# A float32 decoder trunk on one core: another order for the moving operand, and weights moved by 128 bytes

## Chip, cores and metric

The kernel runs on one core of one Trainium2 chip. The metric is the device time of one execution in microseconds, as the median of several runs; lower is better.

## The reference

Two decoder layers over 512 tokens of width 1,024, in float32. Each layer is a token mixer followed by a dense MLP with a squared ReLU, both behind an RMSNorm and added to the residual; one more RMSNorm ends it.

```python
def reference(x, ...):
    for i in range(DEPTH):                       # DEPTH = 2
        h = rmsnorm(x, norm_mix_g[i])
        if i % 2 == 0:  h = chunked_spatial_gating(h, ...)   # in: 1024 -> 2 x 2048, out: 2048 -> 1024
        else:           h = retention(h, ...)                # q, k: 4 heads x 256; v, g: 4 x 512; out: 2048 -> 1024
        x = x + h
        h = rmsnorm(x, norm_ffn_g[i])
        a = jax.nn.relu(h @ mlp_w1[i])                       # 1024 -> 4096
        x = x + (a * a) @ mlp_w2[i]                          # 4096 -> 1024
    return rmsnorm(x, final_norm_g)
```

## The kernel before

**Three matmuls for one product.** Every float32 operand is split into a high part of type float32r and the remainder, `lo = value - hi`. A product is then high x high + high x low + low x high, three matmuls into the same accumulator in PSUM. `mm3` (L213) issues them; L215, L216 and L217 are its lines. With 128 rows, 128 stationary columns and 512 moving columns each, nearly all of TensorE's time is in these three lines.

**Two directions.** Where the result is wanted with features on the partitions (`feat`, `out_piece`: groups `up` and `dn` in layer 1, `u`, `g`, `qk`, `o`, `ro`), the weights are the stationary operand, loaded 128 columns at a time, and 512 tokens of activation move. Where tokens are wanted on the partitions (`tokens`: groups `v`, `vv` and, in the second layer's last products, `dt`), activations are stationary and 512 columns of weights move. In the retention head, `sc` (scores) and `av` (scores times values) have activations on both sides, and 512, 384, 256 or 128 moving columns. Column sums for the norms and their spread over partitions (`stats`, `spread`: groups `st_...`, `bc_...`) have a constant, `onesr`, as the stationary operand and call `matmul` directly. So do the first four pieces of weights (`v0`, L562) and the small transposes (`xt`, `wst`, `tt`) and gating products (`sg`).

**Weights.** All weight matrices are cut into 240 pieces of 128 x 1,024 elements, in the order of use. The queue of SyncE brings in two pieces with a DMA of 1 MB into a `raw` tile. ScalarE copies a piece into `wH` (L179) and VectorE subtracts into `wL` (L183). `prep` does this two to three pieces ahead of TensorE; there are four `wH` tiles, three `wL` tiles and two `raw` tiles. `refill` calls it after each step, so VectorE's and ScalarE's queues hold this work between the evacuations of accumulators. The order of everything is written out by hand as a list of steps.

**Where things lie.** Tiles are allocated one behind another in each partition: the pool `keep` (constants, norms, `xT`, and the normed activations `hH`, `hL`), then `wts` (`raw`, `wH`, `wL`), `bigp` (other activations, ten tiles of 8 KB), `work`. In the built kernel `keep` begins at byte 16,512, `onesr` lies at 17,024, and a tile named `fill`, which nothing uses, puts `xT0` at 24,576. From there on `hH`, `hL`, the weights' tiles and `bigp`'s lie on multiples of 2,048. Both parts of a piece start at the start of their tile.

Of the kernel before, what the change touches and what calls it, by code (L numbers as in the profile page):

```python
# [10 lines left out]
F32 = mybir.dt.float32  # L11
F32R = mybir.dt.float32r
# [5 lines left out]
P = 128  # L18
# [60 lines left out]
def trunk(ctx, tc, x, norm_mix_g, norm_ffn_g, a_w_in, a_b_in, a_v_norm_g, a_w_s, a_b_s, a_w_out,  # L79
# [4 lines left out]
    keep = ctx.enter_context(tc.tile_pool(name="keep", bufs=1))  # L84
    wts = ctx.enter_context(tc.tile_pool(name="wts", bufs=3))
# [28 lines left out]
    ident = keep.tile([P, P], F32, name="ident")  # L114
    onesr = keep.tile([P, P], F32R, name="onesr")
    rows = keep.tile([P, P], F32, name="rows")
    rows2 = keep.tile([16, P], F32, name="rows2")
    gT = keep.tile([P, 80], F32, name="gT")
    wide = keep.tile([P, D], F32, name="wide")
    rbc, r2bc = wide[:, 0:T], wide[:, T:D]  # L120
    r4 = keep.tile([P, NT], F32, name="r4")
    rh4 = keep.tile([P, NT], F32, name="rh4")
    vgh = keep.tile([P, 16], F32, name="vgh")
# [3 lines left out]
    ssf = keep.tile([P, NT, 2], F32, name="ssf")  # L127
    ms0 = keep.tile([P, NT], F32, name="ms0")

    keep.tile([P, 320], F32, name="fill")  # L130
    xT = [keep.tile([P, T], F32, name=f"xT{k}") for k in range(KD)]
    hH = [keep.tile([P, T], F32R, name=f"hH{k}") for k in range(KD)]
    hL = [keep.tile([P, T], F32R, name=f"hL{k}") for k in range(KD)]
# [32 lines left out]

    def prep_tiles(i):
        p = order[i]
        p.hi = wts.tile(p.shape, F32R, tag="wH", name=f"wH{i}", bufs=4)
        p.lo = wts.tile(p.shape, F32R, tag="wL", name=f"wL{i}", bufs=3)  # L170

    def prep(upto, low=None):

        low = upto if low is None else low
        while pos["piece"] < min(upto, len(order)):
            p = order[pos["piece"]]
            load_raws(raws.index(p.raw) + RAW_BUFS)
            prep_tiles(pos["piece"])
            nc.scalar.copy(out=p.hi, in_=p.raw.tile[p.view])  # L179
            pos["piece"] += 1  # L180
        while pos["low"] < min(low, len(order)):
            p = order[pos["low"]]
            nc.vector.tensor_sub(out=p.lo, in0=p.raw.tile[p.view], in1=f32(p.hi))  # L183
            pos["low"] += 1
# [27 lines left out]

    def mm3(ps, ah, al, bh, bl, start, stop):  # L213

        nc.tensor.matmul(ps, lhsT=ah, rhs=bh, start=start, stop=False)  # L215
        nc.tensor.matmul(ps, lhsT=ah, rhs=bl, start=False, stop=False)  # L216
        nc.tensor.matmul(ps, lhsT=al, rhs=bh, start=False, stop=stop)  # L217
# [85 lines left out]
    def mm_f(p, ps, bH, bL, ks, last):  # L303
        for k in ks:
            mm3(ps, p.hi[:, k, :], p.lo[:, k, :], bH[k], bL[k], k == 0, k == last)

    def mm_o(p, t, ps, bH, bL):
        ts = slice(t * P, (t + 1) * P)
        for k in range(4):
            mm3(ps, p.hi[:, k, ts], p.lo[:, k, ts], bH[:, k, :], bL[:, k, :], k == 0, k == 3)  # L310
# [28 lines left out]
    def tokens(plist, bufs, evac, name, behind=None, last=None):  # L339

        accs = {}
        behind = behind or {}

        def one(i):
            def run(p):
                if i == 0:
                    for n in range(NT):
                        accs[n] = acc(f"{name}_{n}")
                aH, aL = bufs()
                for n in range(NT):  # L350
                    s = slice(n * P, (n + 1) * P)
                    for k in range(2):
                        kk = 2 * i + k
                        mm3(accs[n], aH[kk][:, s], aL[kk][:, s], p.hi[:, k, :], p.lo[:, k, :], kk == 0, kk == 7)
                advance()
                refill()
                if i in behind:
                    behind[i]()
                if i == 3:
                    for n in range(NT):  # L360
                        launch(evac(n, accs[n]))
            return run

        for i, p in enumerate(plist[:2] if last else plist):
            step(one(i), p)
        if last:
            step(lambda *ps: last(bufs, accs, evac, *ps), *plist[2:])
# [589 lines left out]
    for _ in range(5):  # L957
        nc.tensor.matmul(warm[:, 0:P], lhsT=ident, rhs=ident, start=True, stop=True)
    columns(rows2, 0, 16)
    prep_tiles(0)  # L960
    for k in range(2):
        p = order[0]
# [56 lines left out]
```

## Time and profile before

| | |
|---|---|
| median of 3 runs | 1406.9 us (1406.83 to 1407.25) |
| the profiled execution | 1407.72 us, of which the span from first to last instruction 1406.0 us |
| granted TensorE clock in it | 0.998 |
| TensorE matmul busy | 1390.5 us (99%) |
| weight loads busy | 1155.4 us (82%) |
| VectorE, ScalarE, GpSimd busy | 793.0, 507.2, 127.7 us |

How to read the rows below: PE is TensorE's matmul row, PEld its weight loads, DVE VectorE, ACT ScalarE, POOL GpSimd, SP SyncE. A row names the line of the kernel, what is written and from what, and the shapes. A matmul's start is measured; its end is modelled, and one starts before the one ahead of it has ended. What a stream of matmuls costs is therefore the distance between starts, not the length of one. A time in front of a row is from the start of the span.

### The profile page before, as it was taken

To read this page: it belongs to the slowest core of one execution; us is meant where nothing else is said; L and a number is where in the kernel's file an instruction comes from. 1 tells how busy PE (TensorE), PEld (TensorE's weight loads), DVE (VectorE), ACT (ScalarE), POOL (GpSimd) and SP (SyncE) were. 2 spreads that over 40 slices of the span, in tenths; PEclk is the share of its full clock that TensorE was granted. 3 is DMA by queue.
4 is the path that set the end of the run, shared out by engine and by line. 5 is a ranking of instruction groups with operands and counts; after the bars stand their busy time and mean duration, and the time that the engine had idled before them with its cause. 6 is when DMAs were issued, how large, how long until landed. Compare 5 with 4: busy or idle time off the path is not lost.

```text
span 1406.0 us, 15372 instructions
## 1 busy us (share of the span) xinstructions
PE 1390.5 (99%) x6290; PEld 1155.4 (82%) x6290; DVE 793.0 (56%) x1102; ACT 507.2 (36%) x721; POOL 127.7 (9%) x98
## 2 busy tenths in 40 slices
PE   8999999999999999999999999999999999999997
PEld 7888888888888888888888888888888888888885
DVE  6757765775444445476647574564685443434335
ACT  4656633334413223123334323333334422313222
POOL 3010111220000000011111100110130000000002
PEclk9999999999999999999999999999999999999999
DMA  6332222232223322423222131132122332232221
GB/s 225 109 116 90 72 90 88 81 120 90 90 90 104 106 90 90 148 89 108 90 78 72 60 120 60 62 118 90 61 90 91 120 104 90 93 117 91 90 90 60
DMA packets 106101, 135.23 MB, mean 96 GB/s; under 512 B 2400, under 2 KB 79792, under 8 KB 105776
## 3 DMA queue, kind: packets, MB, share of 16 engines
q1 hardware_dynamic: 106000, 134.26, 29.4%
q8 instruction: 49, 0.80, 0.2%
q14 instruction: 20, 0.16, 0.0%
q10 hardware_dynamic: 32, 0.01, 0.0%
HBM read 132.16 MB, written 2.10 MB: 95 GB/s over the span
## 4 chain that ended last, share of the span: by engine, by line
PE 96%; DVE 3%; POOL 0%; ACT 0%; DMA 0%; issue 0%; SPq 0%; ACTq 0%; DVEq 0%
PE up L217 8%; PE up L216 8%; PE up L215 8%; PE dn L217 4%; PE dn L216 4%; PE dn L215 4%; PE dt L216 4%; PE dt L217 4%; PE dt L215 4%; PE g L215 2%; PE qk L215 2%; PE vv L216 2%; PE g L216 2%; PE vv L215 2%; PE g L217 2%; PE vv L217 2%
## 5 line engine op out<-in xcount | busy, mean ns | idle before, releaser
L183 DVE TENSOR_TENSOR wL<-raw,wH 128x1024 fp32r<-128x1024 f32 x239 | 305.9, 1282 | 112.8 <-PE dt L216 65.5
L179 ACT CAST wH<-raw 128x1024 fp32r<-128x1024 f32 x239 | 249.7, 1045 | 264.7 <-PE dt L217 114.9
L215 PE MATMUL up<-hH,wH 128*128 128x512 f32 x480 | 187.2, 390 | 0.0
L217 PE MATMUL up<-hH,wL 128*128 128x512 f32 x480 | 186.8, 389 | 0.0
L216 PE MATMUL up<-hL,wH 128*128 128x512 f32 x480 | 186.8, 389 | 0.0
L631 DVE TENSOR_TENSOR aH<-r 128x512 fp32r<-128x512 f32 x64 | 45.0, 703 | 159.5 <-ACT r L629 159.4
L216 PEld LDWEIGHTS up<-hL,wH 128*128 128x128 f32 x480 | 90.1, 188 | 18.7
L215 PEld LDWEIGHTS up<-hH,wH 128*128 128x128 f32 x480 | 90.1, 188 | 18.7
L217 PEld LDWEIGHTS up<-hH,wL 128*128 128x128 f32 x480 | 90.1, 188 | 18.7
L215 PE MATMUL dn<-aH,wH 128*128 128x512 f32 x256 | 99.6, 389 | 0.0
L216 PE MATMUL dn<-aL,wH 128*128 128x512 f32 x256 | 99.6, 389 | 0.0
L217 PE MATMUL dn<-aH,wL 128*128 128x512 f32 x256 | 99.6, 389 | 0.0
L215 PE MATMUL dt<-wH,aH 128*128 128x512 f32 x256 | 99.6, 389 | 0.0
L216 PE MATMUL dt<-wL,aH 128*128 128x512 f32 x256 | 99.6, 389 | 0.0
L217 PE MATMUL dt<-wH,aL 128*128 128x512 f32 x256 | 99.6, 389 | 0.0
L629 ACT ACTIVATE r<-up 128x512 f32<-128x512 f32 x60 | 35.9, 598 | 166.7 <-PE up L217 166.7
L239 POOL TENSOR_TENSOR ssq<-ssq,sq 128x512 f32<-128x512 f32 x28 | 43.0, 1537 | 401.6 <-ACT sq L238 401.3
L501 DVE TENSOR_TENSOR xs<-dn,wide 128x512 f32<-128x512 f32 x32 | 22.1, 692 | 74.5 <-PE dn L217 74.5
L215 PEld LDWEIGHTS dt<-wH,aH 128*128 128x128 f32 x256 | 48.0, 188 | 10.1
L216 PEld LDWEIGHTS dn<-aL,wH 128*128 128x128 f32 x256 | 48.0, 188 | 10.0
L215 PEld LDWEIGHTS dn<-aH,wH 128*128 128x128 f32 x256 | 48.0, 188 | 10.0
L216 PEld LDWEIGHTS dt<-wL,aH 128*128 128x128 f32 x256 | 48.0, 188 | 9.9
(271 smaller groups left out, 2709.5 us busy)
## 6 DMA issues: line engine op xcount, KB each, us to landing
raw<-in_mlp_w_dram SPq DMA_DIRECT2D x64, 1024.0 KB, 5.1
raw<-in_b_w_in_dram SPq DMA_DIRECT2D x24, 1024.0 KB, 5.0
raw<-in_a_w_in_dram SPq DMA_DIRECT2D x14, 1024.0 KB, 5.2
raw<-in_a_w_out_dram SPq DMA_DIRECT2D x8, 1024.0 KB, 4.9
raw<-in_b_w_out_dram SPq DMA_DIRECT2D x8, 1024.0 KB, 4.9
raw<-in_a_w_in_dram SPq DMA_DIRECT2D x8, 256.0 KB, 6.7
out_dram<-out SPq DMA_DIRECT2D x8, 256.0 KB, 2.1
xr<-in_x_dram SPq DMA_DIRECT2D x3, 512.0 KB, 6.6
```

What stands on the lines that cost most here:

```text
L179: nc.scalar.copy(out=p.hi, in_=p.raw.tile[p.view])
L183: nc.vector.tensor_sub(out=p.lo, in0=p.raw.tile[p.view], in1=f32(p.hi))
L215: nc.tensor.matmul(ps, lhsT=ah, rhs=bh, start=start, stop=False)
L216: nc.tensor.matmul(ps, lhsT=ah, rhs=bl, start=False, stop=False)
L217: nc.tensor.matmul(ps, lhsT=al, rhs=bh, start=False, stop=stop)
L239: nc.gpsimd.tensor_tensor(out=state["ssq"], in0=state["ssq"], in1=sq, op=ALU.add)
L501: nc.vector.tensor_mul(t, ps, r2bc)
L629: nc.scalar.activation(r, ps, AF.Relu)
L631: nc.vector.tensor_mul(h, r, r)
```

## The change

In `mm3`, where the moving operand has 512 columns, the access patterns of the moving operand and of the output get two more levels: 64 groups, 2 halves, 4 columns. Columns pass in the order 0 to 3, 256 to 259, 4 to 7, 260 to 263 and so on: 16 bytes from the first 1,024 bytes of a row, 16 from the second. The output is addressed in the same order, so each column's result is where it was.

`wH` and `wL` tiles become 64 elements longer, 4,352 bytes in all, and a piece's part stands in the middle, 32 elements or 128 bytes from the tile's start. To make room, `rows2` (used once at the start, for turning the norms' gains) becomes a view of `wide`, and `fill` shrinks from 320 to 192 elements. With that `xT`, `hH` and `hL` begin 1,024 bytes earlier, `xT0` at 23,552, a multiple of 1,024; the weights' tiles, and `bigp` at 119,552, lie on multiples of 256.

```diff
-    rows2 = keep.tile([16, P], F32, name="rows2")
...
     rbc, r2bc = wide[:, 0:T], wide[:, T:D]
+    rows2 = wide[0:16, 0:P]
...
-    keep.tile([P, 320], F32, name="fill")
+    keep.tile([P, 192], F32, name="fill")
...
     def prep_tiles(i):
         p = order[i]
-        p.hi = wts.tile(p.shape, F32R, tag="wH", name=f"wH{i}", bufs=4)
-        p.lo = wts.tile(p.shape, F32R, tag="wL", name=f"wL{i}", bufs=3)
+        hi = wts.tile([P, 1024 + 64], F32R, tag="wH", name=f"wH{i}", bufs=4)
+        lo = wts.tile([P, 1024 + 64], F32R, tag="wL", name=f"wL{i}", bufs=3)
+        p.hi, p.lo = (t[:, 32 : 32 + 1024].rearrange("p (a b) -> p a b", a=p.shape[1]) for t in (hi, lo))
...
     def mm3(ps, ah, al, bh, bl, start, stop):
+        if bh.shape[1] == 512:
+            ps, bh, bl = (v.rearrange("p (h l f) -> p l h f", h=2, f=4) for v in (ps, bh, bl))
         nc.tensor.matmul(ps, lhsT=ah, rhs=bh, start=start, stop=False)
         nc.tensor.matmul(ps, lhsT=ah, rhs=bl, start=False, stop=False)
         nc.tensor.matmul(ps, lhsT=al, rhs=bh, start=False, stop=stop)
```

## The prediction

> **What bounds the kernel now.** I read the page first: the busy times, the chain that ended last, the costliest groups.
>
> ```profile
> span 1406.0 us, 15372 instructions
> PE 1390.5 (99%) x6290; PEld 1155.4 (82%) x6290; DVE 793.0 (56%) x1102; ACT 507.2 (36%) x721; POOL 127.7 (9%) x98
> PE 96%; DVE 3%; POOL 0%; ACT 0%; DMA 0%; issue 0%; SPq 0%; ACTq 0%; DVEq 0%
> L183 DVE TENSOR_TENSOR wL<-raw,wH 128x1024 fp32r<-128x1024 f32 x239 | 305.9, 1282 | 112.8 <-PE dt L216 65.5
> L179 ACT CAST wH<-raw 128x1024 fp32r<-128x1024 f32 x239 | 249.7, 1045 | 264.7 <-PE dt L217 114.9
> L215 PE MATMUL up<-hH,wH 128*128 128x512 f32 x480 | 187.2, 390 | 0.0
> ```
>
> TensorE (PE) is the chain: 96% of it. No other engine is near its limit over the whole. So the question is what one matmul costs. The 390 ns of the group row is the modelled length of one, not its price: they overlap. The price is the distance between two starts, which the timeline shows, with the weight loads of the same stretch behind it:
>
> ```profile
> 499.98 0.39 PE L217 MATMUL dn<-aH,wL 128*128 128x512 f32 x1
> 500.20 0.39 PE L215 MATMUL dn<-aH,wH 128*128 128x512 f32 x1
> 500.43 0.39 PE L216 MATMUL dn<-aL,wH 128*128 128x512 f32 x1
> 500.66 0.39 PE L217 MATMUL dn<-aH,wL 128*128 128x512 f32 x1
> ...
> 500.43 0.19 PEld L217 LDWEIGHTS dn<-aH,wL 128*128 128x128 f32 x1
> 500.66 0.19 PEld L215 LDWEIGHTS dn<-aH,wH 128*128 128x128 f32 x1
> ```
>
> Three starts take 0.68 us, 226.7 ns each, and the load for the next matmul begins with the present one, every time. The same over long stretches, in the view that cuts the span into windows (length, PE busy, count; then PEld, DVE, ACT, POOL; clock, DMA share, GB/s):
>
> ```profile
> 314.00:652.00 338.00, 338.00 (x1492) 279.79 (x1491) 177.72 (x217) 103.69 (x132) 12.73 (x8) 1.00 0.31 103
> 1010.00:1098.00 88.00, 87.96 (x404) 72.91 (x404) 64.26 (x90) 37.99 (x56) 11.95 (x8) 1.00 0.32 102
> ```
>
> 338.00 us over 1,491 loads is 226.7 ns a matmul, though the stretch mixes weights that are a piece of the matrix with moving activations, from several pools.
>
> How much of 226.7 ns is the 512 columns? The retention head has matmuls of fewer columns in one run:
>
> ```profile
> 716.68 0.39 PE L215 MATMUL av<-pH,vvH 128*128 128x512 f32 x1
> ...
> 717.36 0.33 PE L215 MATMUL av<-pH,vvH 128*128 128x384 f32 x1
> ...
> 717.88 0.29 PE L215 MATMUL av<-pH,vvH 128*128 128x256 f32 x1
> ...
> 718.25 0.22 PE L215 MATMUL av<-pH,vvH 128*128 128x128 f32 x1
> ```
>
> Three matmuls of 512 columns take 0.68 us, three of 384 take 0.52, three of 256 take 0.37. From 512 to 384 that is (680 - 520)/(3 x 128) = 0.417 ns a column, so 512 columns are 213.3 ns and **13.3 ns of every matmul are something else**. That remainder is not a constant. Where the column sums of the second layer's norm go through TensorE, with the weights `onesr`:
>
> ```profile
> 651.85 0.40 PE L271 MATMUL st_mix<-st_mix,onesr 128*128 128x512 f32 x1
> 652.09 0.40 PE L272 MATMUL st_mix<-st_mix,onesr 128*128 128x512 f32 x1
> 652.33 0.40 PE L215 MATMUL vv<-wH,hH 128*128 128x512 f32 x1
> ...
> 653.26 0.39 PE L216 MATMUL vv<-wL,hH 128*128 128x512 f32 x1
> 653.49 0.40 PE L217 MATMUL vv<-wH,hL 128*128 128x512 f32 x1
> 653.73 0.39 PE L215 MATMUL vv<-wH,hH 128*128 128x512 f32 x1
> 653.95 0.40 PE L216 MATMUL vv<-wL,hH 128*128 128x512 f32 x1
> ```
>
> Here starts lie 240 and 240 ns apart, later 230, 240 and 220, all at the same size, with no wait named, and at a granted clock that is 1.00 in both windows above. So the remainder runs from about 7 to 27 ns (rows are rounded to 10) with where operands lie or how the load's reads fall against the running matmul's. Its top, 240 - 213.3 = 26.7 ns, is 0.83 ns for each of the 32 pieces of 16 bytes in a load of 128 float32 columns; the usual 13.3 ns is that for half of them. I read it as the load's reads holding up the moving operand's when both go to the same part of the memory.
>
> **The change part by part.**
>
> *The order of reading.* Two rows give the pace of a load, where loads are what limits (eight matmuls of 128 columns each; start, length, what):
>
> ```profile
> 69.78 0.87 PE wst L415 x8
> 130.51 0.89 PE sg L474 x8
> ```
>
> That is 109 and 111 ns for a load of 128 columns, some 0.83 ns a column: 16 bytes in 3.3 ns. The moving operand passes 16 bytes in 4 columns, 1.7 ns, twice as fast. So its walk laps the load's and, wherever they start, is in step with it about half the time: the 13.3 ns. In the new order each half advances 16 bytes per 8 columns, 3.3 ns: the load's own pace. The halves lie 1,024 bytes apart, so both stand at the same place modulo 256. From then on the distance between walk and load stays what it was at the start, and that is set by the addresses.
>
> *The 128 bytes.* Weights' parts now begin 128 past a multiple of 256, activations on one; one of the two is always stationary and the other moving, so the distance is 128 modulo 256 in all projections. If the memory is split so that addresses 128 apart never meet, the load's reads cost nothing. The price of a matmul then lies between 213.3 ns (columns alone) and 240 (every piece meets). I take 216 ns: 213.3 plus what remains over a load's 128 x 0.83 = 106.7 ns in the 109 ns row, some 2.3 ns per instruction. [...]
>
> *How many.* `mm3` gets 240 pieces of weights (the 239 of the group rows and the first, which is split by hand) with 24 matmuls each, less the 96 of the first four pieces, which are written out elsewhere: 5,664. With the 512-column ones of scores (24) and values (48): 5,736. All are on the chain. At 226.7 - 216 = 10.7 ns: **-61.4 us**. In the 72 of the retention head both operands are activations, so the distance is 0, which would be the worst one: up to 72 x 13.3 = +1.0 us. The 96 written out keep their order but meet a 128 offset: between -1.3 and +1.3 us, taken as 0. Sums over columns (`onesr`) stay.
>
> *The output.* The matmul's columns go to PSUM in the same order, so every value lands in its old column and readers are untouched. But TensorE now writes runs of 16 bytes, 1,024 apart. No row here shows such a write, nor such a read; bounds are 0 and, if each of the 128 runs cost one column, 128 x 0.417 = 53 ns a matmul. I take 0: four columns a run keep each 16 bytes together, and nothing in the rows points to a price per run. [...]
>
> *What becomes late.* A piece lasts 24 x 226.7 = 5.44 us and would last 5.18. In it VectorE owes 1.28 us and ScalarE 1.05 for the next piece. The fullest stage, 1010 to 1098, has VectorE busy 64.26 of 88 us, 73%; at the same work in 84 us 77%. DMA goes from a share of 0.32 to 0.34. Cover stays. Where TensorE waits for a VectorE chain, it will arrive earlier (first TensorE's waits, then three rows of the chain that ended last):
>
> ```profile
> PE xt L397 <- DMA xr<-in_x_dram: 1.8, 1, 1.8
> PE bc_h L290 <- DVE dg_h L286: 0.9, 3, 0.3
> ...
> 47.49 0.24 PE bc_mix L290
> ...
> 796.80 0.28 PE ro L215
> ...
> 808.58 0.47 PE bc_h L290
> ```
>
> Three heads wait 0.3 us each, 11.8 us after their first `ro` matmul (796.80 to 808.58); 5% off that adds at most 0.6 us each, since part of it is the chain's own: +1.5 us. The two operations that write the parts (1282 and 1045 ns) still write 1,024 elements in a row; should the offset cost them something, idle time ahead of them hides 112.8/239 = 0.47 us each on VectorE and 264.7/239 = 1.1 on ScalarE. Without that cover 10 ns on each would be 2.4 us.
>
> *The rest.* `rows2` now lies in `wide`. It is read at the start, and `wide` gets its next writer only after the first spread of a norm at 47.49 us: 0. Were the first load into it to come late, it would lengthen the 1.8 us that the first transposes wait for the input, by no more than that again. The fill of 192 in place of 320 and the missing `rows2` move activations from a multiple of 8,192 to one of 1,024: all still multiples of 256. Between nothing and the whole gain, in the rivals.
>
> **Sum.** -61.4 + 1.0 + 1.5 = -58.9, say -59 us. The profiled execution took 1407.7 us (span 1406.0 and 1.7 around it), 0.8 above the median of 1406.9. That gives a profiled 1348.8 and a median of about **1348 us**.
>
> **Rivals.**
>
> *Partly away (1370 to 1404 us).* Walk and load do not begin at the same place: a fixed lag of some ns, or a stall that shifts it, uses up part of the 26.7 ns that 128 bytes last at 3.3 ns per 16. Any price from 219.5 to 226 ns. For it: the 220 to 240 ns above show that the remainder moves in small steps. Half the gain: 1407 - 30 = 1377.
>
> *Nothing happens (1405 to 1409).* The remainder belongs to something that neither order nor offset touches, such as the hand-over between loads and matmuls. For it: 226.7 ns over 338 us whatever the tiles. Against it: 220 to 240 at unchanged size. 1406.9. [...]
>
> *Slower: the lock falls on the wrong place.* Once walk and load keep step they can also meet always: then each matmul costs the 240 ns seen with `onesr`, whose place (byte 17,024) is itself 128 past a multiple of 256. 5,736 x 13.3 = +76 us, 1483. It decides as soon as more than half of the 32 pieces meet. In a weaker form matmuls never settle, as after 652.33, about 231 ns: +25 us, 1432.
>
> *Slower: short runs cost.* Each run pays for reading or writing apart: at one column time a run +53 ns, +306 us, 1713 us. It cancels the gain from 10.7 ns a matmul, 0.08 ns a run.
>
> **How the numbers follow.** The whole gain (1333, at 213.3 ns with both extra costs, to 1370, at 219.5): 0.45. Partly: 0.18. Nothing: 0.12. Lock wrong or unsettled: 0.15, about half below 1436. Runs cost: 0.10. The range 1333 to 1436 leaves out some 0.18; the likeliest case's own is 1333 to 1370. A measurement tells 0.2%, 3 us, from no change. Faster 0.63, same 0.12, slower 0.25.
>
> **What would show it.** In a stage of projections starts 216 ns apart, and the window of the first layer's up and down products 1,491 matmuls in 322 us rather than 338; `onesr` matmuls still near 240; the weight loads' starts still on the matmuls'. 226.7 ns again is the third case, 240 the fourth, 250 and more the fifth. I am wrong if the 13.3 ns are not the load's reads, if the lag between load and walk is over a few ns, or if VectorE's waits grow by more than some us.

## The result: 9% slower

The changed kernel takes 1537.2 us (median of four runs, 1536.97 to 1537.81) against 1407.1 for the kernel before on the same chip: ratio 1.092 [1.090, 1.094], +130 us. The prediction was 1348 us. The profiled execution took 1537.2 us, with a span of 1535.1 and the clock at 0.998, as before. One execution of the later kernel `alt1_bare` took 2857 us (span 2855.2, granted clock 1.000), 2.1 times the others, for a reason that was not found, and is left out of that kernel's time.

The page after: span, busy times, the chain that ended last, and the two groups that write the weights' parts.

```profile
span 1535.1 us, 15430 instructions
PE 1521.3 (99%) x6290; PEld 1171.0 (76%) x6290; DVE 792.3 (52%) x1102; ACT 514.8 (34%) x721; POOL 126.6 (8%) x98
PE 98%; POOL 0%; DVE 0%; DMA 0%; ACT 0%; issue 0%; SPq 0%; ACTq 0%
L184 DVE TENSOR_TENSOR wL<-raw,wH 128x1024 fp32r<-128x1024 f32 x239 | 305.5, 1279 | 138.8 <-PE dt L220 75.9
L180 ACT CAST wH<-raw 128x1024 fp32r<-128x1024 f32 x239 | 254.7, 1066 | 304.5 <-PE dt L221 129.8
```

Still 6,290 matmuls, the same work on the other engines, more idle time ahead of them, and a chain that is TensorE alone. The timeline of TensorE in a stage of projections, and a window of 360 us in the first layer's up and down products:

```profile
500.21 0.42 PE L221 MATMUL up<-hH,wL 128*128 128x512 f32 x1
500.46 0.41 PE L219 MATMUL up<-hH,wH 128*128 128x512 f32 x1
500.71 0.42 PE L220 MATMUL up<-hL,wH 128*128 128x512 f32 x1
...
340.00:700.00 360.00, 360.00 (x1442) 274.34 (x1441) 170.94 (x211) 102.24 (x128) 9.43 (x6) 1.00 0.28 91
```

Starts lie 250 ns apart (360.00 / 1,441 = 249.8) where they lay 226.7, with no wait between them. 5,736 matmuls x 23.3 ns = +134 us; the span grew by 129. The prediction had named this size: "250 and more" was its fifth case, that short runs cost. Open are: is it the order or the places, the reading or the writing, and what the 13.3 ns are on which everything was built.

### The profile page after: what moved, and what is told of

It reads as the page before. It is cut to its first block, busy times and chain, and to the rows that moved or that the text cites. A ratio compares the mean times of both kernels' runs of the same rounds, so it can differ in the third digit from the quotient of the medians.

```text
span 1535.1 us, 15430 instructions
## 1 busy us (share of the span) xinstructions
PE 1521.3 (99%) x6290; PEld 1171.0 (76%) x6290; DVE 792.3 (52%) x1102; ACT 514.8 (34%) x721; POOL 126.6 (8%) x98
## 4 chain that ended last, share of the span: by engine, by line
PE 98%; POOL 0%; DVE 0%; DMA 0%; ACT 0%; issue 0%; SPq 0%; ACTq 0%
PE up L220 8%; PE up L221 8%; PE up L219 8%; PE dt L221 4%; PE dt L219 4%; PE dn L221 4%; PE dn L219 4%; PE dn L220 4%; PE dt L220 4%; PE g L219 2%; PE ro L219 2%; PE qk L219 2%; PE u L220 2%; PE u L219 2%; PE o L220 2%; PE o L219 2%
## 5 line engine op out<-in xcount | busy, mean ns | idle before, releaser
L184 DVE TENSOR_TENSOR wL<-raw,wH 128x1024 fp32r<-128x1024 f32 x239 | 305.5, 1279 | 138.8 <-PE dt L220 75.9
L219 PE MATMUL up<-hH,wH 128*128 128x512 f32 x480 | 199.8, 416 | 0.0
L220 PE MATMUL up<-hL,wH 128*128 128x512 f32 x480 | 199.4, 415 | 0.0
L221 PE MATMUL up<-hH,wL 128*128 128x512 f32 x480 | 199.4, 415 | 0.0
L221 PE MATMUL dt<-wH,aL 128*128 128x512 f32 x256 | 106.4, 416 | 0.0
L219 PE MATMUL dt<-wH,aH 128*128 128x512 f32 x256 | 106.4, 416 | 0.0
L221 PE MATMUL dn<-aH,wL 128*128 128x512 f32 x256 | 106.4, 416 | 0.0
L220 PE MATMUL dn<-aL,wH 128*128 128x512 f32 x256 | 106.4, 416 | 0.0
L219 PE MATMUL dn<-aH,wH 128*128 128x512 f32 x256 | 106.4, 416 | 0.0
L221 PEld LDWEIGHTS dt<-wH,aL 128*128 128x128 f32 x256 | 48.8, 190 | 15.3
L221 PEld LDWEIGHTS dn<-aH,wL 128*128 128x128 f32 x256 | 48.8, 190 | 15.2
```

## Experiments

### One half of the change at a time

`order_only` is the kernel before with the order alone:

```diff
+        if bh.shape[1] == 512:
+            ps, bh, bl = (v.rearrange("p (h l f) -> p l h f", h=2, f=4) for v in (ps, bh, bl))
```

> The order of reading alone; weights' parts and all else where they lay before. Theory 'runs cost' (each of the 128 runs of 16 bytes has a price of its own, whatever the addresses): the 250 ns between starts of the changed kernel come back, 1530 to 1540 us. Theory 'lock on the wrong place' (the loads' reads keep step with the moving operand's and meet at a distance of 128 bytes): at distance 0 the price is another one, 213 to 240 ns between starts, 1335 to 1485 us.

Measured: 1537.5 us, ratio 1.093 [1.091, 1.095]. The order alone gives all of it.

`offset_only` is the changed kernel without those two lines: weights 128 bytes off, columns in plain order.

> The places alone (parts 128 bytes off, rows2 in wide, smaller fill); the moving operand is read in its old order. Both theories put the cause in the order, so near 226.7 ns and 1405 to 1412 us. If places alone disturb the steady 226.7 ns, as after the onesr matmuls, some 230 ns and 1420 to 1435 us.

Measured: 1438.1 us, ratio 1.022 [1.020, 1.023]. The places alone cost 31 us; that is above both ranges that were expected. The two prices don't add up: under the new order the 128 bytes no longer cost anything (1537.2 us with them, 1537.5 without).

`read_only` and `write_only` part the order itself: only the moving operand (`bh`, `bl`), or only the output (`ps`), passes in the new order. In both, results land in other columns than they should.

```diff
+        if bh.shape[1] == 512:                                                             # read_only
+            bh, bl = (v.rearrange("p (h l f) -> p l h f", h=2, f=4) for v in (bh, bl))
...
+        if bh.shape[1] == 512:                                                             # write_only
+            ps = ps.rearrange("p (h l f) -> p l h f", h=2, f=4)
```

> The kernel before, with the moving operand alone read in the new order and the output written straight on; columns of results come out exchanged. 'The read costs': 250 ns between starts and 1537 us, as with both. [...]

> The kernel before, with the output alone addressed in the new order; columns of results come out exchanged. 'The read costs': 226.7 ns and 1407 us. 'The write costs': 1537 us.

Measured: `read_only` 1536.2 us, ratio 1.092 [1.089, 1.095]; `write_only` 1407.5 us, ratio 1.000 [0.999, 1.002]. TensorE's timeline in the first, then in the second:

```profile
500.07 0.41 PE L219 MATMUL up<-hH,wL 128*128 128x512 f32 x1
500.31 0.42 PE L217 MATMUL up<-hH,wH 128*128 128x512 f32 x1
500.57 0.41 PE L218 MATMUL up<-hL,wH 128*128 128x512 f32 x1
```

```profile
499.94 0.39 PE L218 MATMUL dn<-aL,wH 128*128 128x512 f32 x1
500.17 0.39 PE L219 MATMUL dn<-aH,wL 128*128 128x512 f32 x1
500.39 0.39 PE L217 MATMUL dn<-aH,wH 128*128 128x512 f32 x1
```

Two starts take 0.50 us in the one, 0.45 in the other, as before. The price is one of reading; writing PSUM in these runs of 16 bytes costs nothing here (1407.5 us against 1407.0).

### Blocks of matmuls: distance, and length of the runs

The next kernels leave out the trunk. They run blocks of 48 or 72 matmuls of 128 x 128 x 512 into one accumulator, issued as `mm3` does, and differ in one thing from block to block (in outline, without the flags for the first and last matmul):

```python
for wh, wl in pieces:                                  # 8 of 128 columns, repeated 2 or 3 times
    matmul(o, lhsT=wh, rhs=hi); matmul(o, lhsT=wh, rhs=lo); matmul(o, lhsT=wl, rhs=hi)
```

In the chain of waits a block is one row: start, length, name, line, count. Length by count is the pitch, the distance between two starts; the kernel's 226.7 ns comes back in it, so a block stands for the kernel.

`sweep_d` moves the weights in steps of 16 bytes from 0 to 496 past a multiple of 256, in plain order (`seq`) and the new one (`alt`).

> Nothing of the trunk is computed; x is copied to the output. 64 blocks of 72 matmuls of 128 rows, 128 stationary and 512 moving columns, in mm3's pattern, with weights 0, 16, ... 496 bytes past a multiple of 2048 and the moving operand on one; once in the plain order (seq), once in the new one (alt). 'Runs cost': alt is 250 ns at every distance, seq 226 to 240. 'Lock on the wrong place': alt swings with the distance, between about 214 and 250 ns, and some distances are faster than seq.

```profile
24.45 16.32 PE seq_aa L54 x72
40.77 18.02 PE alt_aa L54 x72
58.79 16.80 PE seq_ab L54 x72
...
285.13 18.70 PE alt_ah L54 x72
303.83 16.74 PE seq_ai L54 x72
320.57 18.02 PE alt_ai L54 x72
```

At distance 0 (`aa`) 226.7 and 250 ns; at 16 bytes (`ab`) plain order 233.3; at 128 (`ai`) 232.5 and 250. Plain order has some 227 only at 0 and 256 and 229 to 234 elsewhere; the new one 260 at 112 bytes (`ah`), its worst, and never less than 246. No distance frees it of its price, which ends the two "lock" rivals, and 0, which the prediction took for the worst place, is the best. At 128 bytes plain order is 232.5 - 226.7 = 5.8 ns dearer; times 5,736 that is 33 us, and `offset_only` cost 31.

`sweep_f` splits reading from writing in the blocks, and changes the length of the runs (`f`), the distance of the halves and the number of stationary columns; `_z` has distance 0, `_h` 128.

> Nothing of the trunk is computed. Blocks as in the sweep of distances, at distance 0 and at 128 bytes: only the read reordered, only the write reordered, runs of 2 to 256 columns, 64 and 32 stationary columns, four parts in place of two, halves further apart, 256 moving columns. 'Runs cost in the write': write-only gives 250 ns, read-only 226.7. 'Runs cost in the read' or 'lock': the other way round. Of these two, a price per run would fall in proportion with longer runs (36.7 ns beyond the columns at 4 columns, 18 at 8, 9 at 16) and stay with fewer stationary columns; the lock would fall with the stationary columns (a quarter of the remainder at 32).

```profile
39.86 18.01 PE both_z L54 x72
57.87 18.00 PE read_z L54 x72
75.87 16.36 PE write_z L54 x72
92.23 24.47 PE runii_z L54 x72
...
168.54 16.36 PE runlxiv_z L54 x72
```

The kernels' verdict again: 250, 250 and 227 ns. Runs of 2, 4, 8, 16 and 32 columns give 340, 250, 243, 240 and 237; from 64 columns on the price is gone. A price per run was to fall in proportion, to 18 and 9 ns beyond the columns' 213.3 at 8 and 16 columns a run; 30 and 27 were measured, so it isn't one price per run either. Moving the halves 16 to 128 bytes further apart gives 251 to 240, 256 or 512 bytes 250 again. With a half or a quarter of the stationary columns the new order stays at 247: a first sign against the loads.

### Are the loads the cause at all?

`sweep_g` shrinks the stationary operand to one column (`_one`), for several gaps between the halves (`gap_..`), and to a half, a quarter and an eighth (`p_` plain, `a_` new order, `q_` plain with the weights 128 bytes off).

> Nothing of the trunk is computed. Blocks of 48 matmuls with 128 stationary columns (full) and with one (one), so that next to nothing is loaded. Theory 'load': the 13.3 ns beyond 512 columns and the further 23.3 of the new order are the loads' reads in the moving operand's way; with one stationary column plain is 214 to 216 ns and both vanish. Theory 'own walk': the price lies in the order of the moving operand's own reads; with one column the new order still costs some 20 ns, and it depends on where two successive reads of 16 bytes lie modulo 256: worst at the same place (halves 1024 bytes apart), nothing where they lie far apart (128 bytes). In the blocks 'step', 16 bytes are read every 32 to 256 bytes: 'own walk' gives a large price at 256 (always the same place) and a smaller one at 128 or 64; 'a price per jump' gives the same at all.

```profile
24.39 10.88 PE plain_full L75 x48
35.27 12.01 PE gap_full_aa L75 x48
...
821.20 11.12 PE p_one L75 x48
...
843.44 11.94 PE a_one L75 x48
```

A load of one column reads 1/128 of a full one. If loads were the 13.3 ns, plain order would fall to about 213; it rises to 231.7. The new order has 250 with full loads and 248.8 with one column. **Neither price is the loads'; both stay with the moving operand.** That settles the failed premise. 'Own walk' missed in one point: it left nothing to pay where the halves lie 128 bytes further apart, but with one stationary column no gap of 16 to 240 bytes comes under 240 ns.

`sweep_s` varies the number of moving columns, and where the moving operand lies as well as the weights.

> Nothing of the trunk is computed. Blocks of 48 matmuls: 448 to 64 moving columns with 128, 32 and one stationary columns; the moving operand 0 to 256 bytes off, with weights 0 to 256 bytes off; runs of 2 to 64 columns with one stationary column. If the 13.3 ns are a fixed price of changing from one matmul to the next, they stand at every length and with one column. If they are the loads' reads, they vanish with one column. If what counts is the distance between weights and moving operand, equal offsets of both give 226.7; if each has to lie on a multiple of 256, only 0 and 256 do.

```profile
52.50 8.35 PE nf_full L75 x48
...
69.17 8.39 PE nf_one L75 x48
...
98.69 5.76 PE nd_full L75 x48
...
110.10 5.60 PE nd_one L75 x48
```

With one stationary column, 512 (`p_one` above), 384 (`nf`), 256 (`nd`) and 128 moving columns take 231.7, 175, 116.7 and 60 ns: the remainder beyond 0.417 ns a column is 18.3, 15, 10 and 6.7. It grows with the columns, as a price of reading them would. With 128 stationary columns it doesn't: 13.3, 14 and 13.3 ns at 512, 384 and 256. How a full load and the plain order work together stays open.

The place matters only with full loads. Some 227 ns were measured where both operands lie alike modulo 256 at 64 and 64, 128 and 128, 0 and 256 bytes, and in two near cases (moving operand at 0 and weights at 16, 32 and 16); 231 at 16 and 16, and 229 to 234 elsewhere. Even 0 and 0 took 229 in this kernel, against 226.7 in the other float32 kernels of blocks. With one stationary column it is 231 to 232 at every place tried. So at 512 columns a full load at the right place shortens plain order by some 5 ns, and at a wrong one lengthens it by less than 3.

### Which order is free?

`sweep_p` has blocks of 16 bytes, one every s bytes (`step`; `ab` is 16, `ac` 32, and so on), columns taken in turn from two halves in runs of 1, 2 and 4 (`alti`, `altii`, `altiv`), and blocks in which all matmuls read the same columns (`same`) or, with 256 columns, go on with the next ones or jump 4,096 bytes (`next`, `jump`).

> Nothing of the trunk is computed. Blocks of 48 matmuls, with 128 stationary columns and with one: 16 bytes read every 16, 32, ... 512 bytes; runs of 4, 8 and 16 bytes taken alternately from the two halves; the same 512 columns each time; 256 columns that go on where the last matmul ended, or jump. 'Own walk': with one stationary column the price follows the step, with a pattern that repeats every 256 bytes, from some 224 ns to 320 (at 96 bytes), and steps that are multiples of 256 are among the dear ones. 'A price per jump': one price for all steps but 16. If the 13.3 ns of the plain order belong to the change from one matmul to the next, 'next' is cheaper than 'jump'.

```profile
68.32 10.89 PE step_full_ad L75 x48
...
138.40 15.36 PE step_full_ag L75 x48
...
787.75 10.36 PE alti_full L75 x48
798.11 10.36 PE alti_one L75 x48
808.47 16.02 PE altii_full L75 x48
```

Steps of 48 bytes (`ad`) cost 226.9 ns, of 96 (`ag`) 320, of 128 254.6, of 256 286.9, with a period of 256 (352 bytes, `aw`, take 320 again). All of these read four columns of every 16 bytes; which 16 bytes come next decides. `next` and `jump` both take 120 ns, so where the next matmul's columns begin isn't the price. And **one column from each half in turn takes 215.8 ns**, with one stationary column or 128. That is the pitch that the prediction forecast, in an order that jumps at every column; runs of two take 334.

`sweep_b` repeats this with bfloat16 operands at the same byte addresses, two columns to 4 bytes.

> Nothing of the trunk is computed. The same with bfloat16 operands at the same addresses in bytes, so 16 bytes are 8 columns and the moving operand is read at half the bytes in the same time. If the price lies in how fast reads of 16 bytes follow one another, the plain order comes to 214 to 217 ns and the alternate order by 16 bytes close to it. If it lies in columns, patterns or the change between matmuls, 227 and 250 ns or nearly so.

```profile
44.39 10.36 PE plain_full L75 x48
...
65.11 13.01 PE altii_full L75 x48
78.12 10.88 PE altiv_full L75 x48
89.00 10.36 PE altviii_full L75 x48
...
182.24 10.36 PE step_full_g L75 x48
```

Plain order, a distance of 128 (`off`), runs of 16 bytes (`altviii`), and steps of 96 bytes: 215.8 ns all. Runs of 8 bytes cost 226.7, of 4 bytes 271. With bfloat16, 16 bytes last eight columns; with float32 in plain order four.

One picture fits, the author's inference from these pitches: even and odd columns would be fetched by two paths, and a path would be free if its column stays within the same 16 bytes for eight columns' time. In the order by single columns (215.8 ns) each path would walk one half and have its 16 bytes for eight columns; in plain float32 order (226.7) both would need new ones every four. That two groups of 16 bytes are in use at once isn't enough: runs of two columns also use just two for eight columns, and cost 334 ns; there each path would go to and fro between both.

### The kernel with the free order

Three kernels carry these orders into the trunk. `run64` is `order_only` with runs of 64 columns (`f=64`). `alt1_bare` takes single columns from the halves and writes them straight on, so results stay in the exchanged order:

```diff
+        if bh.shape[1] == 512:
+            ps = ps.rearrange("p (l h) -> p l h", h=2)
+            bh, bl = (v.rearrange("p (h l) -> p l h", h=2) for v in (bh, bl))
```

`alt1` does the same in the projections, and in the four pieces of `v0`, but not in `sc` and `av`; whoever evacuates an accumulator puts the columns back by reading it in the order of the halves:

```diff
+    def halves(v):
+        return v.rearrange("p (h l) -> p h l", h=2)
+    def turn(v):
+        return halves(v).rearrange("p h l -> p l h")
+    def pairs(v):
+        return v.rearrange("p (l h) -> p l h", h=2)
+    def back(v):
+        return pairs(v).rearrange("p l h -> p h l")
...
+    def mm3(ps, ah, al, bh, bl, start, stop, alt=True):
+        if alt:
+            ps, bh, bl = pairs(ps), turn(bh), turn(bl)
...
-                nc.vector.tensor_add(xT[i], xT[i], ps)
+                nc.vector.tensor_add(halves(xT[i]), halves(xT[i]), back(ps))   # and so in every evacuation of a projection
```

> The kernel before with the new order in runs of 64 columns, 256 bytes, in place of 4; the whole is computed. By the sweep of runs such a run costs nothing: 226.7 ns and 1405 to 1410 us. If the number of levels of the access pattern or any alternation had a price, more than 1420 us.

> The kernel before; the moving operand read column by column in turn from its two halves (4 bytes each, in place of 16), the output written straight on and not put back in order, so that columns of results come out exchanged. The blocks with this order took 215.8 ns a matmul. If that holds beside the other engines: 1406.8 - 5,736 x 10.8 ns = 1345 us, and some 1.5 us for longer waits. If the block's price came of something that the kernel lacks: 1407 us.

> The same order, with the accumulators read back in order by VectorE and ScalarE (every second column, 8 bytes apart, in two sweeps), so that the whole is computed; also in the first four pieces, not in scores and values. 5,760 matmuls at 215.8 ns: 1344 to 1348 us, if reading every second column of PSUM costs VectorE and ScalarE nothing that TensorE waits for. If such reads take twice the time, some 0.5 us more per accumulator on VectorE, its busiest stage comes near 90% and 1350 to 1370 us follow.

Measured: `run64` 1407.6 us, ratio 1.000 [0.999, 1.002]: long runs cost nothing and gain nothing. `alt1_bare` 1345.3 us (median of three runs), ratio 0.956 [0.954, 0.957]. `alt1`, which computes the whole reference, **1346.4 us (five runs, 1345.72 to 1346.59), ratio 0.957 [0.955, 0.958]**: faster than both kernels. Its span, timeline, a window, TensorE's longest wait and one of the evacuations; below them that evacuation in the kernel before:

```profile
span 1344.9 us, 15436 instructions
...
500.21 0.38 PE L229 MATMUL up<-hH,wH 128*128 128x512 f32 x1
500.43 0.38 PE L230 MATMUL up<-hL,wH 128*128 128x512 f32 x1
500.65 0.38 PE L231 MATMUL up<-hH,wL 128*128 128x512 f32 x1
...
340.00:620.00 280.00, 280.00 (x1299) 245.35 (x1298) 153.69 (x177) 84.83 (x105) 12.67 (x8) 1.00 0.32 107
...
PE bc_h L304 <- DVE dg_h L300: 2.3, 3, 0.8
...
L515 DVE TENSOR_TENSOR xs<-dn,wide 128x512 f32<-128x512 f32 x32 | 22.1, 692 | 66.3 <-PE dn L231 66.3
```

```profile
L501 DVE TENSOR_TENSOR xs<-dn,wide 128x512 f32<-128x512 f32 x32 | 22.1, 692 | 74.5 <-PE dn L217 74.5
```

280.00 / 1,298 = 215.7 ns a matmul. 5,760 of them (5,736, less 72, plus 96) at 226.7 - 215.8 = 10.9 ns are -62.8 us; the three heads' waits give back 1.4; the span is 61.1 shorter. Reading every second column of an accumulator costs VectorE nothing here: 692 ns in both.

### A test of the two paths

`sweep_e` asks the picture for orders that it had not been made from. Rival: the gain comes from two separate walks, each through its own half.

> Nothing of the trunk is computed. Blocks of 48 matmuls. Theory 'two paths': even and odd columns of the moving operand are fetched apart, and a fetch costs nothing where each stays with its 16 bytes for 8 columns' time. Then two columns c apart in turn, in blocks of 2 c (near), give 215.8 ns for every c from 4 on and more than 225 for c = 2; four or more parts column by column (parts) give 300 ns and more; every second column (every ii) too; the place of the weights (alt_z to alt_p) changes nothing. Theory 'two walks': only walks that lie a multiple of 256 bytes apart run free; near is 215.8 from c = 64 on and dearer below, and halves 1024 bytes and 16 to 128 more apart (gap) are dearer.

```profile
96.81 10.36 PE alt_h L119 x48
107.17 10.36 PE altone_h L119 x48
...
169.34 13.60 PE partsiv L119 x48
...
290.85 10.90 PE nearii L119 x48
301.75 10.36 PE neariv L119 x48
...
436.43 21.76 PE everyii L119 x48
```

Columns only 4 apart in turn (`neariv`: 0, 4, 1, 5, ...) are as good as the halves, 215.8 ns; 2 apart (`nearii`), where each path would need new bytes every four columns, 227, the plain price. Four parts in turn (`partsiv`), where each path would go to and fro between two walks, 283, less than the 300 that were expected. Every second column (`everyii`), 16 bytes for only two, 453. The place of the weights (`alt_h`: 128) changes nothing, nor does one stationary column: 215.8 ns both. Two walks far apart aren't needed, so that rival falls; the picture of two paths holds for these pitches, but for the size of `partsiv`. It remains an inference: no row shows a path. It doesn't explain all: plain order, the steps and the changed kernel all have four columns to 16 bytes and cost from 224 to 320 ns, by where the next 16 bytes lie. Why 96 bytes are the dearest stays open.

## Why the prediction was wrong, point by point

**The bound** was read rightly: TensorE's pitch is the price. `alt1` and the change both move the time by the number of matmuls times the pitch, within 5 us, and the count of 5,736 holds. After the change the rows in which VectorE ended last are gone from the chain (3% to 0%), and TensorE's waits on `bc_h` with them; that some of those stretches took up the slower matmuls would explain the 5 us, but was not tried.

**The step that failed: "I read it as the load's reads holding up the moving operand's".** The split into 213.3 ns of columns and 13.3 of something else was right, and the remainder did change with places. But loads of one column leave it standing (231.7 ns), and the best place is the one taken for the worst. What the runs showed in the loads' place is the order in which the moving operand itself is read: that alone takes the pitch from 226.7 to 215.8 ns or to 250. The row that decided for the prediction, `onesr` at 240 ns, showed that the remainder varies, not which of two readers pays; no place in the blocks brought plain order to 240 (234 at most), so those two rows stay unexplained. The profile before could not part the readers, since all its matmuls of 512 moving columns load 128 stationary ones; and bounds of 213.3 to 240 were put around a cause, not around the operation. A full load still counts in plain order: 226.7 to 234 ns by its place, against 231 to 232 with one column.

**The order of reading** rested on walks that keep step with loads, so it had no term for a price of its own on the reading side: nothing was taken for the 128 jumps, +23.3 ns was measured. The fifth case, "each run pays for reading or writing apart" (10%, 1713 us), had the sign, and half of the cause: reading costs (`read_only`, 1536.2 us), writing doesn't (`write_only`, 1407.5). Its price per run doesn't hold. Beyond the plain 226.7 ns, 128 runs of 4 columns cost 23.3 ns, 0.18 ns each, between the 0.08 at which they were to cancel the gain and the 0.417 of the bound; but 16 runs of 32 cost 10 ns, 0.6 each.

**The 128 bytes** were to keep the loads' reads out of the way; alone they cost 31 us (`offset_only`), since 0 is the best distance and not the worst (226.7 ns against 232.5 at 128, `sweep_d`). That kernel also has the activations 1,024 bytes lower, for which the prediction allowed "between nothing and the whole gain" and which no kernel did alone. The blocks, which moved only the weights, give 33 us, so nothing need be left for it.

**The output at nothing** was right: `write_only` has the same runs of 16 bytes and takes 1407.5 us, ratio 1.000, and the block with the output alone reordered (`write_z`) 227 ns.

**The small terms.** `bc_h`'s waits went from 0.9 to 2.3 us in `alt1`: +1.4, where +1.5 was forecast for this pitch. The 72 matmuls of the retention head belong to the 23.3 ns like the others. The offset cost the operations that write the parts nothing (1,279 ns against 1,282 on VectorE; on ScalarE 1,042 in `offset_only` against 1,045). The 96 of `v0`, in plain order at the new distance, went in undisturbed stretches from 225 to 228 ns to 230 to 235: some 0.6 us, inside the 1.3 that were allowed. In the likeliest case's range, 219.5 ns comes to 1368 us by the same sum, not 1370; nothing hangs on it.

**The target itself was real, and that is luck.** 216 ns was forecast and 215.8 measured, -59 us forecast and -61 measured, but in another order and for another reason. The 2.3 ns per instruction in the 216 were taken from loads at 0.83 ns a column. No run shows that term: the rows' 109 and 111 ns for 128 columns are 0.85 and 0.87 ns a column, which leaves nothing over. The runs showed in its place the 2.5 ns that the bfloat16 blocks keep beyond the columns at 512, 256 and 128 columns (215.8, 109.2 and 55.8 ns), so of the 13.3 some 10.9 are the order of reading. The 215.8 ns, which no row of before showed, were measured with bfloat16 in nearly any order, with float32 only where single columns alternate.

## What to carry to other kernels

Before a remainder of some ns is put down to one of two readers, shrink one of them to a single column in a block of 48 matmuls: that is one run. With float32r operands on a TensorE-bound kernel such as this, let the moving columns alternate between two places (halves as in `alt1`, or four columns apart as in the block `neariv`), write the accumulator straight on and put the columns back when it is evacuated: 215.8 ns in place of 226.7 for 512 columns here. In float32r, runs of 2 to 32 columns (340 to 237 ns), and steps of 96 or 256 bytes between 16-byte groups (320 and 287), are to be avoided.

## What was not expected of the hardware

- A moving operand's pitch depends on its own addresses: float32r, 512 columns, from 215.8 ns (alternating columns) over 226.7 (plain) to 453 (every second column) and 640 (`everyxii`, every twelfth, 30.72 us for 48).
- Plain order is 5 ns dearer with one stationary column (231.7) than with 128 at the right place (226.7).
- The new order of TensorE's reading slows ScalarE's copies into `wH`, though nothing of them changed: 1,045 ns before, 1,099 in `read_only`, 1,045 in `write_only`. In the changed kernel it is 1,066. VectorE's operation that writes `wL` keeps its time (1,282 before, 1,279 in the changed kernel). The idle time ahead of the copies, 301.7 / 239 = 1.26 us each in `read_only`, covers the 54 ns.

```profile
L179 ACT CAST wH<-raw 128x1024 fp32r<-128x1024 f32 x239 | 262.5, 1099 | 301.7 <-PE dt L219 128.7 <-PE dn L218 113.0 <-PE o L218 13.4
```
